# One product for v of both head pairs, the gate's rank-16 input in fp32 quarters, and attention of both pairs chunk by chunk

## The chip, the cores and the metric

The kernel runs on one core of a Trainium2 chip. The metric is the device time of one execution in microseconds (us); lower is better. A core has a matrix engine (TensorE, PE in the rows; PEld is its weight load), a vector engine (VectorE, DVE), an activation engine (ScalarE, ACT), GpSimd (POOL) and a queue that issues most DMAs (SyncE, SP). They run beside each other and wait for each other through semaphores. Each engine takes its own instructions strictly in the order in which the program lists them.

## The reference

One layer of a decoder runs over 1024 prompt tokens and 64 sample tokens (8 sequences of 8), 1088 in all. The part that the change touches is gated linear attention, with 4 heads of key width 64 and value width 128:

```python
h = rms_norm(x, norm_g)
proj = jnp.einsum('btd,de->bte', h, w_in.astype(h.dtype))
a, gl, zc, q, k, v, zg, lr = jnp.split(proj, SPLIT_POINTS, axis=-1)
u = a * jax.nn.sigmoid(gl)                       # then a causal depthwise conv, width 31, over u
...
gk = jax.nn.log_sigmoid((jnp.einsum('btr,rk->btk', lr, w_alpha.astype(lr.dtype))
                         + b_alpha.astype(lr.dtype)).astype(jnp.float32)) / GATE_NORM
...                                              # per chunk of tokens, with state S:
bcum = jnp.cumsum(gi, axis=-2)
q_t = qi * jnp.exp(bcum)
k_t = ki * jnp.exp(-bcum)
attn = jnp.where(mask, jnp.einsum('bhtd,bhsd->bhts', q_t, k_t), 0.0)
o = jnp.einsum('bhtd,bhdv->bhtv', q_t, S) + jnp.einsum('bhts,bhsv->bhtv', attn, vi)
S = S * jnp.exp(b_last)[..., None] + jnp.einsum('bhsd,bhsv->bhdv', k_dec, vi)
```

`lr` has 16 columns, `v` has 512, `q` and `k` have 256 each.

## The kernel before, in words

Tokens stand in three chunks of 384, 384 and 320 columns; in the last one 256 are prompt and 64 sample tokens. A matrix product of full accuracy is made of three products in the fast format fp32r: operands are split into a high part `h_` (a copy on ACT) and a low part `l_` (a subtraction on DVE, `split`, L422), and TensorE adds high by high, high by low and low by high. Plain fp32 products are slower and show as two matrix records in the trace.

The work in program order: projections `gl` and `a` of four channel tiles (PSUM tiles `p_gl`, `p_a`); `v` for head pair 0 by nine token tiles (`v_tile`, PSUM `pv`), in which 16 more columns give `lr`; `q` and `k` of pair 0 by chunk with its attention between them; `v` of pair 1; `q`, `k` and attention of pair 1; `zc`, `zg`, the pointwise product `pw` and the output products `ya`, `yc`, `pys`.

`lr` of a token tile is copied into `lrst`, its low part subtracted, transposed by TensorE (`lrtp`, L690) and copied to `lrT`. `gates` (L705) multiplies it by `was` (PSUM `pg`), takes the log-sigmoid on ACT and DVE, a cumulative sum on DVE (`scan`, L718) into `B`, and then exponentials on ACT into `ep` and `em`. `q_chunk` and `k_chunk` multiply these by q and k. `gla_states` (L765) transposes k (`pk`, copied to `kT`), multiplies by v (`px`) and updates the state. `gla_out` (L797) makes the attention matrix (`pa`), masks it (DVE `select`, tile `at`) and adds state and attention products in `po`.

The causal convolution is 31 taps for each of four channel tiles, each tap one DVE instruction over 1024 columns (`cv`, L562), and for the sample tokens 31 small ACT instructions and two DVE reductions per tile (L575, L576). `conv_tick(n)` puts the next n of them into the program at low priority.

The order on each engine is not written by hand: `Program.schedule` runs the list of operations against costs written in the code and takes, whenever an engine is free, the ready operation of lowest number (low-priority ones last). What it decides is fixed in the program; the chip then keeps that order, whatever things really take. Its costs for a reduction and a cumulative sum are those of plain element work:

```python
prog.add("DVE", lambda: V.tensor_tensor_scan(R(out), R(a), R(b), 0.0, ALU.mult, ALU.add), [out], [a, b],
         out.n / 0.96 + 67)
...
prog.add("DVE", lambda: V.tensor_reduce(R(out), R(a), mybir.AxisListType.X, ALU.add), [out], [a],
         a.n / 0.96 + 67)
```

Of the kernel before, what the change touches and what calls it, by code (L numbers as in the profile page):

```python
# [48 lines left out]
ADD_LAG = 5000  # L49
SQ_SUM = (2, 4, 8)  # L50
# [76 lines left out]
class Op:  # L127
    __slots__ = ("eng", "fn", "cost", "lag", "table", "prio", "seq", "deps", "users", "wait", "ready", "tiles",
                 "allocs", "start", "end", "bytes", "name")


class Program:
# [9 lines left out]
    def add(self, eng, fn, outs, ins, cost, table=None, nbytes=0, lag=0):  # L142
        o = Op()
        o.eng, o.fn, o.cost, o.table, o.bytes, o.lag = eng, fn, cost, table, nbytes, lag
        o.seq = len(self.ops)
# [37 lines left out]
    def schedule(self):  # L183
# [26 lines left out]
        done = []  # L210

        def can_alloc(o, t):
            need = {}
            for tl in o.tiles:
                if tl.tag in free_at and tl.slot is None:
                    need.setdefault(tl.tag, []).append(tl.first)
            for tag, firsts in need.items():
                have = sum(1 for f in free_at[tag] if f <= t)
                before = min(bisect_left(pend[tag], min(firsts)), self.reserve.get(tag, 1 << 30))
                if have < len(firsts) + before:  # L220
                    return False
            return True
# [6 lines left out]
        while events:  # L229
# [3 lines left out]
            best = None  # L233
            nxt = None
            for o in avail[e]:
                if o.ready <= t:
                    if (best is None or o.prio < best.prio) and can_alloc(o, t):
                        best = o
                elif nxt is None or o.ready < nxt:
# [71 lines left out]
def build(tc, A, O):  # L311
# [3 lines left out]
    prog = Program({"big": NBIG, "unit": NUNIT, "wst": NST, "wl": NW, "wh": NW, "ps": 8, "kT": 2, "S": 6, "ss": 9},  # L315
                   {"ps": 3, "unit": 6, "big": 2})
# [68 lines left out]
    def mm(ps, lhsT, rhs, start, stop, after=(), pair=False):  # L385
# [3 lines left out]
        o = prog.add("PE", lambda: T.matmul(R(ps), R(lhsT), R(rhs), start=start, stop=stop, skip_group_check=True),  # L389
                     [ps], [lhsT, rhs], c / 2 if pair else c, lag=lag)  # L390
# [6 lines left out]
    def transpose(out, in_, idn):  # L397
        return prog.add("PE", lambda: T.transpose(R(out), R(in_), R(idn)), [out], [in_, idn], 109)

    with ctx:  # L400
# [43 lines left out]
        lrst = [VT(fixed, f"lrst{i}", [P, P], F32, f"lrst{i}") for i in range(2)]  # L444
        u_s = [VT(fixed, f"us{i}", [P, NB, CW - 1 + LB], F32, f"us{i}") for i in range(CT)]
        v_s = VT(fixed, "vs", [P, 256], F32, "vs")
# [7 lines left out]
        for t_ in at_p + [at_s] + lrst:  # L454
# [171 lines left out]
        def packed(name, ps, terms):  # L626

            n = len(terms)
            for i, (both, hi, w_h, w_l) in enumerate(terms):
                mm(ps, both, w_h, i == 0, False)  # L630
                mm(ps[0:64], hi, w_l, False, i == n - 1)
            t_ = un(f"half_{name}")
            act(t_[0:64, :ps.n], ps[64:128], AF.Copy)
            return t_


        vt = [[None] * NTT, [None] * NTT]
        lrT = [None] * 3
        hp = VT(big, "big", [P, KT, P], F32R, "hp")

        def v_weights(p):
            cols = 272 if p == 0 else 256
            return cols, [load_split(f"v{p}{i}", A[f"wv{p}"][i], 2, cols) for i in range(4)]

        def v_tile(p, w, tk):
            cols, w = w
            rows = P if tk < 8 else 64
            c = min(tk // 3, 2)
            off = tk * P - CHUNKS[c][0]
            ts_ = slice(off, off + rows)  # L650
            if tk < 8:
                if tk % 4 == 0:
                    vt[p][tk] = VT(big, "big", [P, 4, 256], F32, f"v{p}_{tk}")
                vt[p][tk] = v = vt[p][tk - tk % 4] if tk % 4 else vt[p][tk]
                v = v[:, tk % 4, :]
            else:
                vt[p][8] = v = v_s
            ps = pt(f"pv{p}_{tk}")
            o = ps[:rows, :cols]
            terms = []  # L660
            src = ps[:rows, 256:272]
            if tk < 8:
                for k in range(KT):
                    hi, lo = w[k // 2]
                    terms += [(hh[k][c][:, ts_], hi[:, k % 2, :]), (hh[k][c][:, ts_], lo[:, k % 2, :]),
                              (hl[k][c][:, ts_], hi[:, k % 2, :])]
                accumulate(o, terms)
                act(v[:rows], ps[:rows, 0:256], AF.Copy)
            else:
                for k in range(KT):  # L670
                    hi, lo = w[k // 2]
                    if p == 0:
                        act(hp[:, k, 0:64], hh[k][c][:, 256:320], AF.Copy)
                        act(hp[:, k, 64:128], hl[k][c][:, 256:320], AF.Copy)
                    terms.append((hp[:, k, :], hp[:, k, 0:64], hi[:, k % 2, :], lo[:, k % 2, :]))
                half = packed(f"pv{p}", ps[:, :cols], terms)
                tt(v[:rows], ps[:rows, 0:256], half[:rows, 0:256], ALU.add)
                if cols > 256:
                    tt(half[:rows, 256:272], src, half[:rows, 256:272], ALU.add)
                    src = half[:rows, 256:272]  # L680
            if cols > 256:
                st = lrst[tk % 2]
                sv = st.split(64)
                for a in range(2):
                    act(sv[:rows, a, 0:16].bitcast(F32R), src, AF.Copy)
                for a in range(2):
                    tt(sv[:rows, a, 32:48].bitcast(F32R), src, sv[:rows, a, 0:16], ALU.subtract)
                if off == 0:
                    lrT[c] = un(f"lrT{c}", F32R)
                tp = pt(f"lrtp{tk}")  # L690
                transpose(tp[:, :rows], st[:rows, :], ident[:rows, :rows])
                act(lrT[c][:, ts_], tp[:, :rows], AF.Copy)

        def vslice(p, tk):
            return vt[p][tk][:, tk % 4, :] if tk < 8 else v_s
# [9 lines left out]
        def gates(p, c):  # L705
            t0, n = CHUNKS[c]
            pg = pt(f"pg{p}_{c}")
# [9 lines left out]
            B = un(f"B{p}_{c}")  # L717
# [13 lines left out]
            for i in range(np_):  # L731
                ss_ = slice(i * P, i * P + P)
                act(ep[:, ss_], B[:, ss_], AF.Exp, scale=GN, bias=g_nm[p][:, i0 + i:i0 + i + 1])
                act(em[:, ss_], B[:, ss_], AF.Exp, scale=-GN, bias=g_m[p][:, i0 + i:i0 + i + 1])
            act(g_c[p][:, lo:i0 + np_], g_c[p][:, lo:i0 + np_], AF.Exp)
            if c == 2:
                Bs = B[:, m:n].split(LB)
                act(ep[:, m:n], B[:, m:n], AF.Exp, scale=GN)
                act(em[:, m:n], B[:, m:n], AF.Exp, scale=-GN)
                act(g_c[p][:, 8:9], g_d[p][:, 7:8], AF.Exp)  # L740
                act(g_c[p][:, 12:20], Bs[:, :, LB - 1], AF.Exp, scale=GN)
# [23 lines left out]
        def gla_states(p, c):  # L765
# [3 lines left out]
            km = gx[(p, c)][1]  # L769
            pk = pt(f"pk{p}_{c}")  # L770
            for i in range(nt):
                transpose(pk[:, P * i:P * i + P], km[:, P * i:P * i + P], ident)
            kT = un(f"kT{p}_{c}")
            act(kT[:, :m], pk[:, :m], AF.Copy)
# [637 lines left out]
```

## Time and profile before

| what | value |
|---|---|
| median of 3 runs | 470.25 us (469.52 to 470.39) |
| profiled execution, its own time | 470.04 us |
| its span, first to last instruction | 467.9 us |
| TensorE busy | 458.9 us, 98% of the span |
| VectorE busy | 401.1 us, 86% |
| ScalarE busy | 304.4 us, 65% |

The profile is one execution, taken on the core. Busy times of TensorE count overlapping matrix products as one stretch, and the ends of products are modelled, so the pace of a run of products is read from their starts or from the chain of waits. The 2.1 us between the span and the time of the same execution lie outside the instructions.

### The profile page before, as it was taken

To read this page: it belongs to the slowest core of one execution; us is meant where nothing else is said; L and a number is where in the kernel's file an instruction comes from. 1 tells how busy PE (TensorE), PEld (TensorE's weight loads), DVE (VectorE), ACT (ScalarE), POOL (GpSimd) and SP (SyncE) were. 2 spreads that over 40 slices of the span, in tenths; PEclk is the share of its full clock that TensorE was granted. 3 is DMA by queue.
4 is the path that set the end of the run, shared out by engine and by line. 5 is a ranking of instruction groups with operands and counts; after the bars stand their busy time and mean duration, and the time that the engine had idled before them with its cause. 6 is when DMAs were issued, how large, how long until landed. Compare 5 with 4: busy or idle time off the path is not lost.

```text
span 467.9 us, 7864 instructions
## 1 busy us (share of the span) xinstructions
PE 458.9 (98%) x2867; PEld 431.2 (92%) x2867; DVE 401.1 (86%) x634; ACT 304.4 (65%) x780; POOL 19.3 (4%) x39
## 2 busy tenths in 40 slices
PE   8999999999999999999999999999999999999994
PEld 7899999999999999999999999999999988888783
DVE  4999998999999989999888999995548848988674
ACT  6978649926670545685634696544899548878636
POOL 1000000000000000000000000000000023130000
PEclk9999999999999999999999999999999999999998
DMA  8910283313012110022021011102235392386754
GB/s 253 352 57 1 93 205 57 54 51 69 1 59 78 36 56 6 35 73 77 20 71 39 14 47 45 46 22 73 88 78 181 87 228 48 68 182 154 242 174 179
DMA packets 33238, 43.28 MB, mean 92 GB/s; under 512 B 11696, under 2 KB 16560, under 8 KB 33200
## 3 DMA queue, kind: packets, MB, share of 16 engines
q1 hardware_dynamic: 30896, 38.59, 26.5%
q0 software_dynamic: 2304, 4.20, 5.5%
q8 instruction: 22, 0.36, 0.3%
q14 instruction: 16, 0.13, 0.1%
HBM read 36.58 MB, written 6.19 MB: 91 GB/s over the span
## 4 chain that ended last, share of the span: by engine, by line
PE 88%; DMA 4%; DVE 3%; ACT 3%; issue 1%; SPq 1%; DVEq 0%
PE pv L389 11%; PE p_zc L389 10%; PE p_zg L389 10%; PE p_gl L389 8%; PE p_a L389 8%; PE ya L389 7%; PE p_k L389 5%; PE p_q L389 5%; PE pw L389 5%; PE yc L389 5%; PE po L389 2%; PE pys L389 2%; DMA xr<-in_x 1%; DVE xr L343 1%; DMA s_gl<-in_w_in 1%; DMA s_a<-in_w_in 1%
## 5 line engine op out<-in xcount | busy, mean ns | idle before, releaser
L339 DVE SCALAR_TENSOR_TENSOR cv<-u,par,cv 128x1024 f32<-128x1024 f32 x120 | 150.8, 1278 | 0.2
L389 PE MATMUL pv<-h_v,hh 128*128 128x272 f32 (+1 forms) x128 | 37.4, 292 | 0.0
L389 PE MATMUL pv<-h_v,hl 128*128 128x272 f32 (+1 forms) x128 | 37.1, 290 | 0.0
L389 PE MATMUL pv<-l_v,hh 128*128 128x272 f32 (+1 forms) x128 | 36.8, 288 | 0.0
L333 ACT ACTIVATE pr<-us,par 128x64 f32<-128x64 f32 x124 | 32.3, 343 | 2.4 <-DMA us<-in_cc 2.4
L389 PE MATMUL p_gl<-hh,h_gl 128*128 128x384 f32 (+1 forms) x96 | 32.5, 339 | 0.8 <-ACT hh L333 0.8
L389 PE MATMUL p_zc<-hh,h_zc 128*128 128x384 f32 (+1 forms) x96 | 32.0, 333 | 0.0
L389 PE MATMUL p_gl<-hl,h_gl 128*128 128x384 f32 (+1 forms) x96 | 31.7, 330 | 0.2 <-DVE hl L343 0.2
L389 PE MATMUL p_a<-hh,l_a 128*128 128x384 f32 (+1 forms) x96 | 31.8, 331 | 0.0
L389 PE MATMUL p_a<-hh,h_a 128*128 128x384 f32 (+1 forms) x96 | 31.5, 328 | 0.1
L389 PE MATMUL p_zc<-hh,l_zc 128*128 128x384 f32 (+1 forms) x96 | 31.5, 329 | 0.0
L389 PE MATMUL p_zc<-hl,h_zc 128*128 128x384 f32 (+1 forms) x96 | 31.5, 328 | 0.0
L389 PE MATMUL p_gl<-hh,l_gl 128*128 128x384 f32 (+1 forms) x96 | 31.5, 328 | 0.0
L389 PE MATMUL p_zg<-hh,l_zg 128*128 128x384 f32 (+1 forms) x96 | 31.5, 328 | 0.0
L389 PE MATMUL p_zg<-hl,h_zg 128*128 128x384 f32 (+1 forms) x96 | 31.4, 327 | 0.0
L389 PE MATMUL p_zg<-hh,h_zg 128*128 128x384 f32 (+1 forms) x96 | 31.4, 327 | 0.0
L389 PE MATMUL p_a<-hl,h_a 128*128 128x384 f32 (+1 forms) x96 | 31.4, 327 | 0.0
L389 PEld LDWEIGHTS pv<-h_v,hh 128*128 128x128 f32 x128 | 24.1, 188 | 0.6 <-issue 0.2
L389 PEld LDWEIGHTS pv<-h_v,hl 128*128 128x128 f32 x128 | 24.1, 188 | 0.3 <-issue 0.3
L389 PEld LDWEIGHTS pv<-l_v,hh 128*128 128x128 f32 x128 | 24.1, 189 | 0.2
L389 PEld LDWEIGHTS p_gl<-hh,h_gl 128*128 128x128 f32 x96 | 18.1, 189 | 1.7 <-ACT hh L333 1.2
L389 PEld LDWEIGHTS p_gl<-hl,h_gl 128*128 128x128 f32 x96 | 18.2, 189 | 0.9 <-DVE hl L343 0.5
(337 smaller groups left out, 1306.8 us busy)
## 6 DMA issues: line engine op xcount, KB each, us to landing
xr<-in_x SPq DMA_DIRECT2D x16, 256.0 KB, 4.4
out_y<-xr SPq DMA_DIRECT2D x16, 256.0 KB, 2.3
x<-in_xT SPq DMA_DIRECT2D x16, 192.0 KB, 4.5
T<-in_w_out POOLq DMA_DIRECT2D x12, 256.0 KB, 5.1
s_gl<-in_w_in SPq DMA_DIRECT2D x8, 256.0 KB, 4.9
s_a<-in_w_in SPq DMA_DIRECT2D x8, 256.0 KB, 4.1
s_zc<-in_w_in SPq DMA_DIRECT2D x8, 256.0 KB, 2.6
s_zg<-in_w_in SPq DMA_DIRECT2D x8, 256.0 KB, 2.7
```

Source lines behind the costliest of these rows:

```text
L333: return S.activation(R(out), R(in_), func, **kw)
L339: return prog.add("DVE", lambda: V.scalar_tensor_tensor(R(out), R(a), R(s), R(b), op0, op1), [out], [a, s, b], out.n / 0.96 + 67 + 62 * is ...
L343: return prog.add("DVE", lambda: V.tensor_tensor(R(out), R(a), R(b), op), [out], [a, b], out.n / 0.96 + 67)
L389: o = prog.add("PE", lambda: T.matmul(R(ps), R(lhsT), R(rhs), start=start, stop=stop, skip_group_check=True), [ps], [lhsT, rhs], c / 2 if ...
```

## The change

There are four parts.

1. **v in one product.** `v_tile` makes v of both pairs at once, 512 columns per product, in place of 272 (pair 0 with `lr`) and 256 (pair 1). The weights are eight tiles of 512 columns, each loaded by two DMAs.
2. **The gate input.** `gate_rank` computes `lr` in plain fp32: for each of 8 row blocks four products with 32 weight columns (16 of them zero) and 272 token columns, one for each quarter of the tokens, into four groups of 32 PSUM partitions (`pl`). Its weights come by four DMAs of 64-byte runs into `lr_w`. `gate_rows` copies the result to `lrT` by ACT. The 9 transposes and the `lrst` copies are gone.
3. **Attention by chunk.** `gla_states` handles both pairs, `gla_out` and the gates of both pairs follow chunk by chunk, and what was pair 1's later work moves ahead, among `zc`. More convolution taps stand among the v tiles (`conv_tick(4)`).
4. **The order.** The scheduler knows for each TensorE operation whether it is fp32 or fp32r (`kind`), charges 90 ns for a change, and stays with the kind that runs where a ready operation of it is less than `STICK = 60` numbers behind. An fp32r product is charged 14 ns beside its columns, not 2.5.

```diff
+STICK = 60
...
+            if same is not None and same.prio < best.prio + STICK:
+                best = same
...
+            if e == "PE" and o.kind != kind[0]:
+                kind[0] = o.kind
+                cost += 90
...
-    prog = Program({"big": NBIG, "unit": NUNIT, "wst": NST, "wl": NW, "wh": NW, "ps": 8, "kT": 2, "S": 6, "ss": 9},
-                   {"ps": 3, "unit": 6, "big": 2})
+    prog = Program({"big": NBIG, "unit": NUNIT, "wst": NST, "wl": NW, "wh": NW, "ps": 8, "kT": 2, "S": 8, "ss": 9},
+                   {"ps": 3, "unit": 8, "big": 2})
...
-        c = max(n / 2.4 + 2.5, m / 1.2) if R_DT(rhs) else max(n / 1.2 + 2.5, m / 1.2) + max(n / 1.2 if m > 64 else 53, m / 1.2)
+        c = max(n / 2.4 + 14, m / 1.2) if R_DT(rhs) else max(n / 1.2 + 2.5, m / 1.2) + max(n / 1.2 if m > 64 else 53, m / 1.2)
...
+        def gate_rank():
+            w = un("lr_w")[:, 0:256].split(32)
+            prog.hold = True
+            zero(w)
+            for i in range(4):
+                dma(w[:, 2 * i:2 * i + 2, 0:16], A["wv0"][i][:, :, 256:272], late=True)
+            pl = pt("pl")[:, :QT]
+            for k in range(KT):
+                for g in range(4):
+                    mm(pl[32 * g:32 * g + 32], w[:, k, :], rows("x", k, F32)[:, QT * g:QT * g + QT],
+                       k == 0, k == KT - 1, share=4)
+            th, tl = un("lr_h", F32R)[:, :QT], un("lr_l", F32R)[:, :QT]
+            split(th, tl, pl)
...
+                for p in range(2):
+                    dma(st[:, 256 * p:256 * p + 256], A[f"wv{p}"][k // 2][:, k % 2, 0:256])
...
+        gate_rank()
         for ct in (2, 3):
...
+        wv = v_weights()
         for tk in range(NTT):
+            v_tile(wv, tk)
+            conv_tick(4)
+            if tk in (3, 6):
+                gates(tk // 3 - 1, 0)
+        wqk = [(wtile("q", p), wtile("k", p)) for p in range(2)]
+        for c in range(3):
+            for p in range(2):
                 if (p, c) not in gx:
                     gates(p, c)
+            for p in range(2):
+                q_chunk(p, wqk[p][0], c)
                 conv_tick(2)
                 if c > 0:
+                    if p == 0:
+                        gla_states(c - 1)
+                    else:
+                        gla_out(1, c - 1)
+                k_chunk(p, wqk[p][1], c)
                 conv_tick(2)
+                if c > 0 and p == 0:
+                    gla_out(0, c - 1)
```

Where the scheduler then puts things is seen in the built programs. The first place is, on TensorE, the middle of `p_gl2_1`, the second chunk of the projection `gl` of channel tile 2 (`hh`, `hl` are the split activations, `h_gl2`, `l_gl2` the split weights). Before:

```order
L389 MATMUL p_gl2_1_838<-hl3_203,h_gl2_0_630 128x384
L389 MATMUL p_gl2_1_838<-hh3_187,l_gl2_0_691 128x384
L389 MATMUL p_gl2_1_838<-hh4_210,h_gl2_1_657 128x384
L389 MATMUL p_gl2_1_838<-hl4_228,h_gl2_1_657 128x384
L389 MATMUL p_gl2_1_838<-hh4_210,l_gl2_1_700 128x384
```

and in the change:

```order
L403 MATMUL p_gl2_1_841<-hl3_199,h_gl2_0_626 128x384
L403 MATMUL p_gl2_1_841<-hh3_183,l_gl2_0_672 128x384
L403 MATMUL pl_861<-x0_88,lr_w_790 32x272 x4
L403 MATMUL pl_861<-x1_92,lr_w_790 32x272 x4
L403 MATMUL pl_861<-x2_96,lr_w_790 32x272 x4
L403 MATMUL pl_861<-x3_100,lr_w_790 32x272 x4
L403 MATMUL pl_861<-x4_108,lr_w_790 32x272 x4
L403 MATMUL pl_861<-x5_110,lr_w_790 32x272 x4
L403 MATMUL pl_861<-x6_112,lr_w_790 32x272 x4
L403 MATMUL pl_861<-x7_116,lr_w_790 32x272 x4
L403 MATMUL p_gl2_1_841<-hh4_205,h_gl2_1_655 128x384
```

All 32 products `pl` now stand after the first 36 of the 72 products of `gl2`, and the rest of TensorE's work stands behind them. The weights `lr_w` come through the SP queue, whose rows at that time (`us` are the sample tokens' conv caches, `cst` constants, `s_v` staged weights of v) were, before:

```order
L377 DMA us3_795<-in_cc 128x8x30
L377 DMA cst_798<-in_cst 128x960
L377 DMA bm_800<-in_bm 64x8
L377 DMA cst2_802<-in_cst2 128x384
L377 DMA s_v03_818<-in_wv0 128x544
```

and are in the change:

```order
L391 DMA us3_798<-in_cc 128x8x30
L391 DMA cst_800<-in_cst 128x960
L391 DMA bm_803<-in_bm 64x8
L391 DMA cst2_805<-in_cst2 128x384
L391 DMA lr_w_790<-in_wv0 128x2x16 x4
L391 DMA s_v3_820<-in_wv0 128x256
L391 DMA s_v3_820<-in_wv1 128x256
```

The four loads stand in the place of the fourth v load, behind the four conv caches and the constants. The second place is just ahead of the first q product. ACT and DVE make its weights `h_q0_0`, `l_q0_0`; before, DVE's rows there were taps alone (`cv`), while TensorE was still in `gl3`:

```order
L339 SCALAR_TENSOR_TENSOR cv1_830<-u1_294,par_86,cv1_830 128x1024
L339 SCALAR_TENSOR_TENSOR cv0_727<-u0_381,par_86,cv0_727 128x1024
L343 TENSOR_TENSOR l_q0_0_1202<-s_q0_0_945,h_q0_0_1190 128x512
L339 SCALAR_TENSOR_TENSOR cv0_727<-u0_381,par_86,cv0_727 128x1024
L343 TENSOR_TENSOR l_q0_1_1226<-s_q0_1_969,h_q0_1_1208 128x512
```

In the change DVE has the cumulative sum of pair 1's first gates (`ge1_0<-cst,g1_0`) and taps ahead of it:

```order
L353 SCALAR_TENSOR_TENSOR cv1_894<-u1_287,par_86,cv1_894 128x1024
L368 SCALAR_TENSOR_TENSOR ge1_0_1673<-cst_800,g1_0_1680 128x384
L353 SCALAR_TENSOR_TENSOR cv1_894<-u1_287,par_86,cv1_894 128x1024
L353 SCALAR_TENSOR_TENSOR gd1_1717<-ge1_0_1673,gm1_1708 128x3
L353 SCALAR_TENSOR_TENSOR cv2_1494<-u2_985,par_86,cv2_1494 128x1024
L357 TENSOR_TENSOR gc1_1731<-gd1_1717,gm1_1708 128x2
L357 TENSOR_TENSOR l_q0_0_1733<-s_q0_0_1291,h_q0_0_1719 128x512
```

and ACT has what follows from that sum ahead of `h_q0_0`:

```order
L347 ACTIVATE gnm1_1705<-ge1_0_1673 128x3
L347 ACTIVATE gm1_1708<-ge1_0_1673 128x3
L347 ACTIVATE g1_0_1680<-ge1_0_1673,gm1_1708 128x128 x2
L347 ACTIVATE h_q0_0_1719<-s_q0_0_1291 128x512
L347 ACTIVATE g1_0_1680<-ge1_0_1673,gm1_1708 128x128
L347 ACTIVATE h_q0_1_1727<-s_q0_1_1377 128x512
```

The q weights moved from a place in which nothing waited for them soon to one right behind the gates, with the first q product next on TensorE.

The third place is the end of the program, where the last four token tiles (`xr4` to `xr7`, halves `_0` and `_1`) are added to the output products (`ya`), squared and summed on ACT (`ss`) and scaled (the instruction with `fg`). DVE's last rows before:

```order
L343 TENSOR_TENSOR xr5_0_4977<-ya1_4439,xr5_0_4977 128x512
L339 SCALAR_TENSOR_TENSOR xr4_0_4975<-xr4_0_4975,ss4_5055,fg_4416 128x512
L339 SCALAR_TENSOR_TENSOR xr5_0_4977<-xr5_0_4977,ss5_5061,fg_4416 128x512
L343 TENSOR_TENSOR xr6_0_4979<-ya2_4456,xr6_0_4979 128x512
L343 TENSOR_TENSOR xr7_0_4982<-ya3_4470,xr7_0_4982 128x512
```

and in the change:

```order
L353 SCALAR_TENSOR_TENSOR xr4_0_4742<-xr4_0_4742,ss4_4793,fg_4181 128x512
L357 TENSOR_TENSOR xr5_0_4744<-ya1_4204,xr5_0_4744 128x512
L353 SCALAR_TENSOR_TENSOR xr5_0_4744<-xr5_0_4744,ss5_4827,fg_4181 128x512
L357 TENSOR_TENSOR xr6_0_4746<-ya2_4221,xr6_0_4746 128x512
L357 TENSOR_TENSOR xr7_0_4748<-ya3_4235,xr7_0_4748 128x512
```

The addition for tile 5 now stands behind the scaling of tile 4, no longer ahead of it; the additions for tiles 6 and 7 stand as before.

## Rows read from the trace of the kernel before

**Rows 1.** The page: busy time and share of the span, by engine.

```profile
PE 458.9 (98%) x2867; PEld 431.2 (92%) x2867; DVE 401.1 (86%) x634; ACT 304.4 (65%) x780; POOL 19.3 (4%) x39
```

**Rows 2.** A window: length, then busy (instructions) of PE, PEld, DVE, ACT, POOL; clock.

```profile
60.00:108.00 48.00, 48.00 (x293) 48.00 (x292) 46.19 (x47) 30.87 (x110) 0.00 (x0) 1.00 0.39 79
```

**Rows 3.** Chain of waits: start us, us, what, number; the first v stretch.

```profile
108.24 5.67 PE pv L389 x45
113.91 0.11 PE lrtp L398
```

**Rows 4.** Chain of waits over the whole span, three long pieces.

```profile
60.70 11.90 PE p_gl L389 x72
...
197.14 2.84 PE pv L389 x24
...
390.21 10.88 PE ya L389 x48
```

**Rows 5.** Timeline of PE (start, length, what, number) around a state product.

```profile
149.64 0.34 PE L389 MATMUL p_k<-hh,l_k 128*128 128x384 f32 x1
149.91 0.88 PE L389 MATMUL px<-v,kT 128*64 128x128 f32 x12
150.72 0.44 PE L389 MATMUL p_k<-hh,h_k 128*128 128x384 f32 x1
151.00 0.34 PE L389 MATMUL p_k<-hl,h_k 128*128 128x384 f32 x1
```

**Rows 6.** Timeline of SP's queue; start us and us of the issue.

```profile
60.25 4.29 SPq L377 DMA_DIRECT2D us<-in_cc  x4
...
66.55 0.38 SPq L377 DMA_DIRECT2D s_v<-in_wv  x1
```

**Rows 7.** DMA issues from 58 to 80 us: number, size, median us to landing.

```profile
s_v<-in_wv SPq DMA_DIRECT2D x3, 272.0 KB, 2.8
...
us<-in_cc SPq DMA_DIRECT2D x4, 120.0 KB, 4.3
...
bm<-in_bm SPq DMA_DIRECT2D x1, 2.0 KB, 3.8
```

**Rows 8.** Timeline of DVE: taps, a cumulative sum, splits, a reduction, a tap.

```profile
101.69 3.67 DVE L339 SCALAR_TENSOR_TENSOR cv<-u,par,cv 128x1024 f32<-128x1024 f32 x3
...
134.32 0.95 DVE L354 TENSOR_TENSOR_SCAN B<-cst,g 128x384 f32<-128x384 f32 x1
135.19 1.27 DVE L343 TENSOR_TENSOR l_v<-s_v,h_v 128x512 fp32r<-128x512 f32 x2
...
142.36 1.97 DVE L364 TENSOR_REDUCE pr<-pr 128x64 f32<-128x1024 f32 x1
144.25 1.27 DVE L339 SCALAR_TENSOR_TENSOR cv<-u,par,cv 128x1024 f32<-128x1024 f32 x1
```

**Rows 9.** Timeline of ACT: exponentials of the gates, a copy of transposed k.

```profile
138.52 0.39 ACT L333 ACTIVATE ge<-B,gnm 128x128 f32<-128x128 f32 x1
138.82 0.39 ACT L333 ACTIVATE g<-B,gm 128x128 f32<-128x128 f32 x1
...
148.96 0.49 ACT L333 ACTIVATE kT<-pk 128x384 f32<-128x384 f32 x1 [9.17 <-PE pk L398]
```

**Rows 10.** Windows at the end; the last figures are clock, DMA share, GB/s.

```profile
460.90:463.60 2.70, 0.15 (x1) 0.00 (x0) 1.37 (x3) 2.51 (x10) 0.00 (x0) 1.00 0.50 191
463.70:467.90 4.20, 0.00 (x0) 0.00 (x0) 0.63 (x1) 0.60 (x1) 0.00 (x0) 0.50 0.54 208
```

**Rows 11.** Timeline of the end: ACT and DVE on the last token tiles.

```profile
455.69 0.63 ACT L333 ACTIVATE sq<-xr 128x512 bf16<-128x512 f32 x1 [0.60 <-DVE xr L343]
...
456.30 0.68 DVE L343 TENSOR_TENSOR xr<-ya,xr 128x512 f32<-128x512 f32 x1
...
457.01 0.75 DVE L339 SCALAR_TENSOR_TENSOR xr<-xr,ss,fg 128x512 f32<-128x512 f32 x1
...
459.61 0.68 DVE L343 TENSOR_TENSOR xr<-ya,xr 128x512 f32<-128x512 f32 x1
```

More of the change, by code (lines that the diff above doesn't have):

```diff
@@ L128 @@
     __slots__ = ("eng", "fn", "cost", "lag", "table", "prio", "seq", "deps", "users", "wait", "ready", "tiles",
-                 "allocs", "start", "end", "bytes", "name")
+                 "allocs", "start", "end", "bytes", "name", "kind")
 class Program:
@@ L232, in schedule @@
                 continue
-            best = None
+            best = same = None
             nxt = None
@@ L238, in schedule @@
                         best = o
+                    if (e == "PE" and o.kind == kind[0] and (same is None or o.prio < same.prio)
+                            and can_alloc(o, t, True)):
+                        same = o
                 elif nxt is None or o.ready < nxt:
@@ L397, in transpose @@
     def transpose(out, in_, idn):
-        return prog.add("PE", lambda: T.transpose(R(out), R(in_), R(idn)), [out], [in_, idn], 109)
+        return prog.add("PE", lambda: T.transpose(R(out), R(in_), R(idn)), [out], [in_, idn], 109, kind=False)
     with ctx:
@@ L641, in v_weights @@
[L641 to L647, printed above, removed]
+        QT = NTOK // 4
+        lr_parts = []
+        def gate_rank():
[11 more added lines that the diff above has]
+            split(th, tl, pl)
+            lr_parts.extend((th, tl))
@@ new lines, in build, with gate_rows @@
+        lrT = [None] * 3
+        def gate_rows(c):
+            t0, n = CHUNKS[c]
+            lrT[c] = un(f"lrT{c}", F32R)
+            for g in range(4):
+                a, b = max(t0, QT * g), min(t0 + n, QT * g + QT)
+                if a < b:
+                    for i in range(4):
+                        act(lrT[c][32 * i:32 * i + 32, a - t0:b - t0],
+                            lr_parts[i % 2][32 * g:32 * g + 32, a - QT * g:b - QT * g].bitcast(F32), AF.Copy)
+        vt = [None] * NTT
@@ new lines, in build, with v_weights @@
+        hp = VT(big, "big", [P, KT, P], F32R, "hp")
+        def v_weights():
+            out = []
+            for k in range(KT):
+                st = VT(wst, "wst", [P, 512], F32, f"s_v{k}")
+                hi = VT(wh, "wh", [P, 512], F32R, f"h_v{k}")
+                lo = VT(wl, "wl", [P, 512], F32R, f"l_v{k}")
+                for p in range(2):
+                    dma(st[:, 256 * p:256 * p + 256], A[f"wv{p}"][k // 2][:, k % 2, 0:256])
+                split(hi, lo, st)
+                out.append((hi, lo))
+            return out
@@ L648, in v_tile @@
+        def v_tile(w, tk):
             c = min(tk // 3, 2)
             off = tk * P - CHUNKS[c][0]
-            ts_ = slice(off, off + rows)
+            ts_ = slice(off, off + P)
+            ps = pt(f"pv{tk}")
             if tk < 8:
[L652 to L657, printed above, removed]
@@ L675, in v_tile @@
[L675 to L692, printed above, removed]
+                    act(hp[:, k, 0:64], hh[k][c][:, 256:320], AF.Copy)
@@ L1070, in build @@
+        for i in range(4):
+            w = wtile("zc", i)
+            for c in range(3):
+                zc_chunk(i, w, c)
+                conv_tick(5)
+                for f, *args in beside[(i, c)]:
+                    f(*args)
         conv_tick(1000)
```

207 lines of the change are left out of this document (86 added, 121 removed).

## The prediction

> **What bounds the kernel now.** I read the page's busy times first. TensorE is busy for 98% of the span, VectorE for 86% [rows 1]. In a window of the middle, 60 to 108 us, TensorE has no gap at all while VectorE is busy for 46.2 of 48 us [rows 2]: TensorE sets the end, and VectorE runs just behind it with almost no slack. So work taken off TensorE counts in full, and a new wait of TensorE counts in full as well, which VectorE can cause as soon as its work is put in another order. The chain of waits gives the pace of TensorE's products, with long runs of one kind in it. A product of 272 columns takes 5.67/45 = 0.126 us [rows 3], one of 256 2.84/24 = 0.118, one of 512 10.88/48 = 0.227, and `p_gl`, whose chunks are 384, 384 and 320 wide, 11.90 us for 72, in proportion 0.174 for 384 columns and 0.146 for 320 [rows 4]. A plain fp32 transpose of 128 columns stands between two fp32r runs with 0.11 us [rows 3]; no time for a change of precision shows there.
>
> The timeline around a `px` block tells where changes do cost. The block is six fp32 products of 128 by 64, twelve records; from the `p_k` ahead of it to the second one behind it are 151.00 - 149.64 = 1.36 us [rows 5], less two `p_k` of 0.174 leaves 1.01. Twelve records one after the other would take 12 x 0.11 = 1.3 by the transpose, so the two halves run side by side: six steps, 0.66 us, and 0.35 for going into narrow products and out again. The Trainium skill has a rule for that (TensorEngine Tiling (Array Packing), section Key Properties): changing the tiling mode drains TensorE. It is a rule on shapes, not on precision, and the two rows agree with it: 0.35 us around narrow products, nothing seen around the full-size transpose.
>
> **The change part by part.** The sum is made against the profiled execution's own 470.04 us (span 467.9), 0.2 below the median of 470.25.
>
> v in one product: 208 products (192 of the full token tiles, 16 of the last) at 0.227 in place of 208 pairs at 0.126 + 0.118. That is 208 x 0.0175 = -3.6 us, all on TensorE. Bounds -2.6 and -4.6, 5 ns either way on a product.
>
> Transposes of `lr`: eight of full size at 0.11, -0.9.
>
> Attention of both pairs together, and the order that keeps to one precision: precision changes on TensorE fall from 103 to 47 in the built programs, and blocks of narrow products from 24 to 16 beside `pl`. By what these rows show only the blocks count [rows 3, 5]: 8 x 0.35 = -2.8. Below this stands 0, if drains are only moved; above it, if every change costs half a block's 0.35, 56 x 0.175 = -9.8.
>
> `pl` is new: 32 products of 32 output columns over 272 columns of fp32. A step of `px` (one record of each of the two halves, 128 columns) takes 0.11 us by the split above, so a step of 272 columns takes 0.11 x 272/128 = 0.23. If four run at once there are 16 steps (two records each of eight row blocks), 3.7 us, and one block's 0.35: +4.0. Two at a time give +7.7, one at a time 15. I take four, as the two halves of `px` are seen side by side. The Trainium skill speaks against a full factor of four (TensorE: Matmul & The Clock Gate, section Measured speedup vs the span model): three narrow column tiles gained 2.38 and not 3; in proportion `pl` would come to an estimated 4.6 and 0.35, or +4.9, for which no row here stands. TensorE's work is thus -3.6 - 0.9 - 2.8 + 4.0 = -3.3.
>
> The wait at `pl`. It stands behind 36 products of `gl2`: from 60.70 us [rows 4] 36 x 0.174 = 6.3, so TensorE comes to it at 67.0. Its weights `lr_w` are queued on SP behind four cache loads that take 4.3 us to issue, and constants; where they now stand, a v load was issued at 66.55 [rows 6], and one more load half ahead of the caches adds its 0.38 us, so 66.9. Small runs land late: the 2 KB of `bm` after 3.8 us, the caches, of 120-byte runs, after 4.3, the big v loads after 2.8 [rows 7]. `lr_w` has 64-byte runs and is small; I take 3.8, and the first of the four loads lets TensorE start. TensorE waits 66.9 + 3.8 - 67.0 = +3.7 (bounds 2.7 and 4.3 by these rows, 0 if the load gets ahead). Everything behind `pl` on TensorE waits with it, and so does VectorE, whose split of `lr` is in its queue.
>
> The wait at the first q product. From the end of `pl` TensorE has the rest of `gl2` (12 x 0.174 + 24 x 0.146 = 5.6), `a2`, `gl3`, `a3` (3 x 11.9 = 35.7), v (208 x 0.227 = 47.2) and 0.7 for two `pg` and two q products: 89.2 us. VectorE, which must make `l_q0_0` for the third q product, has in its new order 58 taps, four reductions, nine splits, two cumulative sums and 18 smaller instructions between its split of `lr` and `l_q0_0`. From one start to the next a tap takes (3.67 - 1.27)/2 = 1.2, a split 0.6 (two in 1.27), the cumulative sum 0.87 (134.32 to 135.19), the reduction 1.89 (142.36 to 144.25) [rows 8]: 69.3 + 7.6 + 5.4 + 1.7, and some 0.34 for each small one, 6.1, together 90.1 us. It starts about 1 us after `pl`, and 0.2 us pass before TensorE sees the result: +2.1 of waiting. The planner's cost for a reduction is 1.13 and for a sum 0.47; that is why it saw none. With ACT the q weight's high part is queued behind the exponentials' offsets that wait for that sum, which is part of the same 2.1. Bounds 0 and 5 (3% of VectorE's 90 us either way).
>
> The wait at the first state product. TensorE has 146 products of 0.174, two `pg` and six transposes, 26.4 us, from the third q product to `px0_0`. VectorE has ten taps, eight splits, two reductions and some eight smaller ones to the end of the next cumulative sum, 25.5. ACT then has six exponentials at 0.30 (138.52 to 138.82), 0.4 for the long one and 0.3 of small ones, and the copy `kT` of 0.49, which is queued behind them [rows 9]; with 0.4 of latencies 28.9. +2.5; bounds 0 and 4.
>
> Later waits of the same kind (a select ahead of the first `po`, the norm of the first outputs): +1.5 by the same counts, bounds 0 and 3. From there VectorE has the slack of the later stages.
>
> The end. Before, the addition for tile 5 started at 456.30 beside ACT's square of tile 4 (455.69); the scaling of tile 4 came at 457.01. Now that addition follows the scaling: 457.01 + 0.65 = 457.66, 1.4 us later. From an addition to ACT's square behind it pass 0.7, from the square to the scaling 1.32 (455.69 to 457.01), to the next addition 0.65: the addition for tile 6 comes at 460.33, where it was at 459.61 [rows 11]. ACT's chain behind it is the last one, so +0.7 (bounds 0 and 1.4).
>
> Sum: -3.3 + 3.7 + 2.1 + 2.5 + 1.5 + 0.7 = +7.2, so 477.2 on the profiled execution, 477.5 on the median.
>
> **Rivals.** B, the clock falls while TensorE waits. At the end it was at its high level for 2.7 us after the last product and at half from 463.7 [rows 10], while TensorE did nothing; a wait of 3.7 at `pl` is longer than that. No row shows how long it takes to rise again; the row at half covers the last 4.2 us, and as much work at half clock would lose half of that, +2.1: 479.6. Against it: that fall came behind the end of all work, and it would come only just before `lr_w` lands here. The Trainium skill's page on the clock gate (section HAM oscillation — how this bites in real kernels) says that waits for DMAs can throw the clock back each time, which would be this case; no row of before has such a wait.
>
> C, `lr_w` lands in time, since small transfers pass the caches: without 3.7, 473.8.
>
> D, `pl` goes two at a time: +3.7, 481.2.
>
> E, VectorE keeps up (its order has 1% less in it than I count, and the other waits with it): without 2.1 + 2.5 + 1.5, 471.4.
>
> F, the other side: each change of precision costs half of 0.35, whatever the shape. 56 fewer are -9.8 in place of -2.8: 470.5, no change; above 0.2 a change it would be faster. The transpose at 0.11 speaks against it [rows 3].
>
> **How the numbers follow.** A, as summed, 0.36; B 0.24; C 0.10; D 0.07; E 0.10; F 0.05; C and E together (467.7) 0.06; rest 0.02. The time is A's, 477.5. The range goes from E, 471.5, to D, 481.3, which leaves out F, C with E and parts of E and D. A measurement of this kernel can tell about 0.2% (0.94 us) from no change: faster 0.09, same 0.06, slower 0.85.
>
> **What would show it.** In the profile after: `pl` with idle time ahead of it that a DMA `lr_w` ends (3.7), and about 4 us long; v at 0.227 a product in one run of 47 us; idle time of TensorE ahead of `p_q` ended by ACT or VectorE (2.1) and ahead of `px` ended by `kT` (2.5); narrow blocks of both pairs as one; a granted clock under 1.0 behind `pl` for B. The prediction is wrong if TensorE shows no gaps, or if `pl` takes 8 us, or if the full-size blocks turn out to cost what the narrow ones do.

## The result and the profile after

The change makes the kernel slower by more than was forecast: 483.02 us median of 4 runs (482.08 to 488.16) against 469.88 for the kernel before beside it; ratio over all these runs 1.0306, interval 1.023 to 1.0381 (the medians alone give 1.028). The prediction was 477.5, its range ended at 481.3. The profiled execution took 483.29 us with a span of 481.5, 13.6 more than the span of before.

The page's row of busy times, which answers to [rows 1], says at once what kind of loss it is:

```profile
PE 459.8 (95%) x2714; PEld 420.0 (87%) x2714; DVE 397.7 (83%) x615; ACT 306.8 (64%) x769; POOL 19.5 (4%) x38
```

TensorE is busy as long as before (458.9 there), in a span that is 13.6 us longer: it waits. What it waits for is a view of its own (engine, line, what ended the wait: us in total, times, longest):

```profile
PE pl L403 <- DMA lr_w<-in_wv: 3.1, 1, 3.1
PE p_q L403 <- ACT h_q L347: 1.9, 1, 1.9
...
PE on_1p L403 <- DVE on_1l L357: 0.9, 1, 0.9
PE p_q L403 <- DVE l_q L357: 0.9, 1, 0.9
PE px L403 <- ACT kT L347: 0.9, 1, 0.9
...
PE ya L403 <- DVE xr L357: 0.7, 1, 0.7
PE po L403 <- DVE at L375: 0.4, 1, 0.4
```

The forecast places are there: `pl`, q (`p_q`), `px`, and the later ones (`po` behind the select, `on_1p` for the norm of the first outputs). Two more are not forecast: `ya` in the last stage and a small one at `pj_3p`, which isn't shown (0.3). The timeline of TensorE around three of them (columns as in [rows 5]; in brackets idle time and what ended it) lets one measure each from start to start:

```profile
66.49 0.34 PE L403 MATMUL p_gl<-hh,l_gl 128*128 128x384 f32 x1
69.96 5.26 PE L403 MATMUL pl<-x,lr_w 128*32 128x272 f32 x64 [3.14 <-DMA lr_w<-in_wv]
75.15 0.44 PE L403 MATMUL p_gl<-hh,h_gl 128*128 128x384 f32 x1
...
166.22 0.44 PE L403 MATMUL p_q<-hh,h_q 128*128 128x384 f32 x1 [1.93 <-ACT h_q L347]
...
167.75 0.44 PE L403 MATMUL p_q<-hh,l_q 128*128 128x384 f32 x1 [0.92 <-DVE l_q L357]
...
196.83 0.88 PE L403 MATMUL px<-v,kT 128*64 128x128 f32 x12 [0.90 <-ACT kT L347]
```

From 66.49 to 69.96 are 3.47 us, less one product of 0.17: 3.3 of waiting, 3.7 forecast. (The view of waits counts from the modelled end of the last product, and so shows a little less.) `pl` takes 5.19 us, 4.0 forecast. The two waits at q are 2.1 and 1.1, `px` is late by 1.05 more. The granted clock (the last figures but two, after the busy times) explains `pl`, and a slow stretch behind the waits at q:

```profile
68.50:69.00 0.50, 0.00 (x0) 0.00 (x0) 0.50 (x1) 0.00 (x0) 0.00 (x0) 1.00 0.48 75
69.50:70.00 0.50, 0.04 (x4) 0.07 (x6) 0.50 (x1) 0.33 (x2) 0.00 (x0) 0.50 0.20 19
72.50:73.00 0.50, 0.50 (x12) 0.25 (x8) 0.00 (x0) 0.00 (x0) 0.00 (x0) 0.67 1.03 137
168.00:172.00 4.00, 4.00 (x15) 4.00 (x15) 4.00 (x6) 3.59 (x9) 0.00 (x0) 0.57 0.36 131
```

It stands at half (1.2 in place of 2.4 GHz) from 69.5 on, late in the pause, until some way into `pl` at 72.8, and again in most of 168 to 172 (0.57 over 4 us is 3.4 us at half, 1.7 lost). In the kernels below in which `pl` keeps the high clock it takes 3.8 us.

The end grew most. DVE's last additions and scalings (those that answer to [rows 11]):

```profile
467.47 0.68 DVE L357 TENSOR_TENSOR xr<-ya,xr 128x512 f32<-128x512 f32 x1
469.51 0.75 DVE L353 SCALAR_TENSOR_TENSOR xr<-xr,ss,fg 128x512 f32<-128x512 f32 x1 [1.35 <-ACT ss L347]
470.18 0.68 DVE L357 TENSOR_TENSOR xr<-ya,xr 128x512 f32<-128x512 f32 x1
472.21 0.75 DVE L353 SCALAR_TENSOR_TENSOR xr<-xr,ss,fg 128x512 f32<-128x512 f32 x1 [1.35 <-ACT ss L347]
...
476.84 0.75 DVE L353 SCALAR_TENSOR_TENSOR xr<-xr,ss,fg 128x512 f32<-128x512 f32 x1 [1.18 <-ACT ss L347]
```

The order is as forecast: the addition for tile 5 (470.18) behind the scaling of tile 4 (469.51), 2.71 us from one tile to the next. From the addition for tile 4 (467.47) to the last scaling (476.84) are 9.4 us, before 8.6 (454.98 to 463.58): 0.8 more, 0.7 forecast. But the addition for tile 4 now starts 3.4 us ahead of TensorE's last product; before it was 5.7. These are DVE's two rows of before, and TensorE's last rows before and after (the last product starts 0.39, its own length, ahead of the end of its row: 460.66 and 470.83):

```profile
454.98 0.68 DVE L343 TENSOR_TENSOR xr<-ya,xr 128x512 f32<-128x512 f32 x1
463.58 0.75 DVE L339 SCALAR_TENSOR_TENSOR xr<-xr,ss,fg 128x512 f32<-128x512 f32 x1 [1.14 <-ACT ss L333]
450.01 11.04 PE L389 MATMUL ya<-p4b,p4a 128*128 128x512 f32 x48
462.76 8.46 PE L403 MATMUL ya<-p4b,p4a 128*128 128x512 f32 x36 [0.67 <-DVE xr L357]
```

From the last product to the end of the span are 10.7 us, before 7.2. Of the 3.4 more, 0.8 are thus the order, 2.3 the later start against TensorE, 0.3 stand behind the last scaling.

So the 13.6 us: from the start of `gl2` (0.1 earlier than before) to the last product TensorE takes 410.4 us in place of 400.1, and the end 3.4 more. In the 10.3 are 10.4 us of waits (3.3, 2.1, 1.1, 1.05, 0.5 at `po`, 1.1 at `on_1p`, 0.8 at `ya`, 0.45 at `pj_3p`), 1.4 and 1.7 of low clock. What remains is -3.2 for TensorE's own work, -3.3 forecast. The kernel of experiment 8 bears this out: 398.1 us over the same stretch with 1.4 of waiting, so 3.4 of work less than before.

### The profile page after: what moved, and what is told of

Same layout as the page of the kernel before. It is cut to its first block, busy times and chain, and to the rows that moved or that the text cites. A ratio compares the mean times of both kernels' runs of the same rounds, so it can differ in the third digit from the quotient of the medians.

```text
span 481.5 us, 7536 instructions
## 1 busy us (share of the span) xinstructions
PE 459.8 (95%) x2714; PEld 420.0 (87%) x2714; DVE 397.7 (83%) x615; ACT 306.8 (64%) x769; POOL 19.5 (4%) x38
## 4 chain that ended last, share of the span: by engine, by line
PE 51%; DVE 32%; ACT 6%; issue 4%; DMA 3%; SPq 2%; DVEq 0%
DVE cv L353 16%; PE p_zg L403 10%; PE ya L403 8%; PE p_zc L403 8%; PE pw L403 5%; PE yc L403 5%; DVE x L353 2%; PE p_k L403 2%; PE po L403 2%; SPq L391 2%; DVE pr L378 2%; DVE cv L378 2%; PE pys L403 2%; DVE hl L357 2%; PE p_q L403 1%
## 5 line engine op out<-in xcount | busy, mean ns | idle before, releaser
L403 PE MATMUL pv<-h_v,hl 128*128 128x512 f32 x64 | 24.9, 390 | 0.0
L403 PE MATMUL pv<-l_v,hh 128*128 128x512 f32 x64 | 24.9, 389 | 0.0
L403 PE MATMUL pv<-h_v,hh 128*128 128x512 f32 x64 | 24.9, 389 | 0.0
L357 DVE TENSOR_TENSOR o<-o,zg 128x384 f32<-128x384 f32 (+1 forms) x12 | 6.2, 532 | 15.8 <-ACT zg L347 15.8
L403 PEld LDWEIGHTS p_a<-hh,h_a 128*128 128x128 f32 x96 | 18.0, 188 | 1.0 <-ACT h_a L347 1.0
L403 PEld LDWEIGHTS p_gl<-hh,l_gl 128*128 128x128 f32 x96 | 18.0, 188 | 0.6 <-DVE l_gl L357 0.4
```

The source lines that it names most:

```text
L357: return prog.add("DVE", lambda: V.tensor_tensor(R(out), R(a), R(b), op), [out], [a, b], out.n / 0.96 + 67)
```

## The experiments

All times are medians beside runs of the kernel before on the same chip (469.7 to 470.0). The planner is `Program.schedule`; waits are read behind 28 us. Theory from the traces: VectorE is the bound from `pl` to `px`, and the order of its work comes from one number of the planner. Rivals: the load at `pl` and the clock carry the loss; the gates' new place or the rule on precision makes the waits.

**1. The load earlier.** Only SP's order is changed.

```diff
         order = self.schedule()
+        first = next(i for i, o in enumerate(order) if o.eng == "SP" and o.tiles[0].name == "us0")
+        moved = [o for o in order[first:] if o.eng == "SP" and o.tiles[0].name == "lr_w"]
+        order = order[:first] + moved + [o for o in order[first:] if o not in moved]
```

> The changed kernel with its four lr_w loads moved ahead of the four cache loads on SP, every other order kept. Theory (the products pl wait for lr_w, and the pause of TensorE drops its clock to half): pl starts right behind gl2, with no wait (3.3 us less) and at the high clock throughout, 3.5 us long in place of 5.2 (1.7 less); all work behind it comes 5.0 us earlier, 478.0 in place of 483.0. Rival (the low clock in pl has another cause): pl stays 5.2 long, 479.7. Rival (the cache loads, now later, are waited for in turn): no gain, 482 to 483.

483.42 us, ratio 1.0281 (1.0248 to 1.0314): no gain, though the wait at `pl` is gone and `pl` runs at the high clock in 3.8 us. The waits have moved (the two longest in the view of waits, as above):

```profile
PE pv L406 <- DVE l_v L360: 3.3, 2, 2.0
PE px L406 <- ACT kT L350: 2.5, 1, 2.5
```

So the load and the clock at `pl`, which the expectation had as its theory, don't carry the loss by themselves. Why, the two timelines show, ACT's:

```profile
72.71 0.31 ACT L350 ACTIVATE Jr<-cst 128x128 fp32r<-128x128 f32 x1 [7.01 <-DMA cst<-in_cst]
...
75.36 0.38 ACT L350 ACTIVATE lr_h<-pl 128x272 fp32r<-128x272 f32 x1
```

and DVE's:

```profile
75.77 0.44 DVE L360 TENSOR_TENSOR lr_l<-pl,lr_h 128x272 fp32r<-128x272 f32 x1 [4.96 <-ACT lr_h L350]
```

`pl` ends at 71, but ACT's copy `lr_h` of it stands in ACT's queue behind the copy of `Jr`, which waits for the constants, 3 us later than in the changed kernel, and behind ten short instructions more; so VectorE starts on `lr_l` at 75.77. In the changed kernel it does so at 75.72, when `pl` has ended at 75.15:

```profile
75.72 0.44 DVE L357 TENSOR_TENSOR lr_l<-pl,lr_h 128x272 fp32r<-128x272 f32 x1 [5.33 <-ACT lr_h L347]
```

That two different causes end so close to each other is chance. And `px` starts at 196.87 here, 196.83 there, 121.1 us after `lr_l` in both, though TensorE stands at other places in between:

```profile
196.87 0.88 PE L406 MATMUL px<-v,kT 128*64 128x128 f32 x12 [2.48 <-ACT kT L350]
```

**2 and 3. Products in the pauses.** In two kernels spare products, whose results nothing uses, keep TensorE busy in the pause ahead of `pl`, or in the two ahead of q; they wait for nothing new. In the second kernel they alter q's first chunk, so its output is another.

```diff
+        def pad(o, out, n):
+            real, m = o.fn, out.n
+            def fn():
+                for i in range(n):
+                    x = T.matmul(R(out), R(rows("hh", 0, F32R)[:, 0:P]), R(rows("hh", 1, F32R)[:, 0:m]), start=True, stop=True,
+                                 skip_group_check=True)
+                    first = x if i == 0 else first
+                real()
+                return first
+            o.fn = fn
...
+                    if k == g == 0:
+                        pad(prog.last_pe, pl, 25)
...
+                    if name == "q0" and c == 0 and k == 0 and i != 1:
+                        pad(prog.last_pe, ps[:, 384:512], 30 if i == 0 else 14)
```

> The changed kernel with 25 spare products (272 columns, into pl's own PSUM bank ahead of its first product) in the wait ahead of pl; the wait for lr_w itself stays. Theory (the clock falls because TensorE pauses): the granted clock stays at 1.00 there, pl starts as before and takes 3.5 us, 1.7 less: 481.3. Rival (the clock falls for another reason, or the fall costs nothing because VectorE is the bound from there on): 483.0.

> The changed kernel with 30 and 14 spare products of 128 columns (into unused columns of the PSUM bank) in the two waits ahead of the first and the third q product. Theory (VectorE is the bound from pl to the first state product px): the clock stays at 1.00 behind the waits, TensorE comes to px 1.7 us earlier, and waits there 2.7 us in place of 1.0: no gain, 483.0. Rival (TensorE is the bound again behind the q wait): 1.7 less, 481.3.

The first took 482.5 us, 1.0269 (1.0238 to 1.0301), the second 482.57, 1.0271 (1.0232 to 1.0311): neither differs from the changed kernel. In the first the clock held and `pl` took 3.8 us, but in that execution the loads were issued 1.1 us later (67.57 against 66.49) and `pl` started 1.0 later, so `lr_l` came only 0.4 earlier (DVE, then TensorE):

```profile
75.31 0.44 DVE L357 TENSOR_TENSOR lr_l<-pl,lr_h 128x272 fp32r<-128x272 f32 x1 [3.87 <-ACT lr_h L347]
```

```profile
196.43 0.88 PE L403 MATMUL px<-v,kT 128*64 128x128 f32 x12 [0.91 <-ACT kT L347]
```

In the second the pause ahead of `pl` was not filled, and this time the clock didn't fall in it (its windows from 66.9 to 70 and behind q):

```profile
66.90:70.00 3.10, 0.16 (x1) 0.00 (x1) 3.06 (x4) 0.27 (x2) 0.00 (x0) 1.00 0.65 193
168.00:172.00 4.00, 4.00 (x25) 4.00 (x25) 4.00 (x6) 2.38 (x5) 0.00 (x0) 1.00 0.33 104
```

`lr_l` came 1.3 us earlier than in the changed kernel, and `px` too (DVE, then TensorE):

```profile
74.39 0.44 DVE L357 TENSOR_TENSOR lr_l<-pl,lr_h 128x272 fp32r<-128x272 f32 x1 [3.77 <-ACT lr_h L347]
```

```profile
195.50 0.88 PE L403 MATMUL px<-v,kT 128*64 128x128 f32 x12 [0.94 <-ACT kT L347]
```

The second kernel is no clean test of the clock behind q: the clock held, but the spare products ran past the pauses. The third q product starts at 168.03, 2.3 us behind the start of DVE's split `l_q` (165.70), in the changed kernel 0.7 (167.75, 167.02). These 1.6 us are about what the clock gave back, so TensorE's wait at `px` stayed at 1.1 us where 2.7 were expected. The clean case is experiment 1: there the clock is high behind q, TensorE waits 2.65 us at `px` (start to start), and `px` comes no earlier. From `lr_l` to `px` are 121.11 us in the changed kernel, 121.10, 121.12 and 121.11 in these three, whatever TensorE does between.

**4. Three taps less.** VectorE's last three taps ahead of its first instruction on `g1_0` (pair 1's first gates) are left out, so the convolution of one channel tile lacks three taps.

```diff
+        dve = [o for o in order if o.eng == "DVE"]
+        at = next(i for i, o in enumerate(dve) if any(t.name == "g1_0" for t in o.tiles))
+        out = dve[at - 3:at]
...
+        order = [o for o in order if o not in out]
```

> The changed kernel without the last three convolution taps ahead of the second gates (3 x 1.2 us of VectorE; the convolution of one channel tile lacks three taps), every order kept. Theory (VectorE, not the load at pl, sets the time of the first q product and of the first state product px): the waits ahead of q shrink from 3.2 us to nothing and px comes 3.6 us earlier, as does all behind it: 479.4. Rival (ACT's order or the load at pl is what TensorE waits for): px and the end stay, 483.

480.36 us, 1.0216 (1.0193 to 1.0239). `lr_l` and `px` (DVE, then TensorE):

```profile
75.87 0.44 DVE L362 TENSOR_TENSOR lr_l<-pl,lr_h 128x272 fp32r<-128x272 f32 x1 [5.55 <-ACT lr_h L352]
```

```profile
193.39 1.16 PE L408 MATMUL px<-v,kT 128*64 128x128 f32 x12 [2.24 <-ACT kT L352]
```

117.52 us: 3.59 less, three taps of 1.2. The waits at q are gone, the one at `px` is 2.2; the span is 3.3 shorter. VectorE's queue is shown to be the bound there: work taken out of it, and nothing else, brings `px` forward by as much.

**5. The planner's number.** Two kernels with one number exchanged: the change with 2.5 ns, and the kernel before with 14.

```diff
-        c = max(n / 2.4 + 14, m / 1.2) if R_DT(rhs) else ...
+        c = max(n / 2.4 + 2.5, m / 1.2) if R_DT(rhs) else ...
```

> The changed kernel with one number of the planner put back: an fp32r product is charged 2.5 ns beside its columns and not 14. Theory (the higher charge lets the planner put more VectorE work, taps above all, ahead of what TensorE needs, and so makes the waits at q, px, the norms and in the tail): these waits go, 3.2 + 1.0 + 1.9 + 4.0 = 10.1 us; the wait at pl (2.6 to 3.4) with its low clock stays: 473 (471 to 475). Rival (the order comes from keeping to one precision and from the gates' new place): waits and time stay, 481 to 485.

471.8 us, 1.0043 (1.0023 to 1.0064): one number gives back 11.2 of the 13.1 us. One wait of TensorE is left, and the end is 7.1 us again, from the last product at 461.91 (windows):

```profile
PE pl L403 <- DMA lr_w<-in_wv: 2.2, 1, 2.2
```

```profile
462.00:469.00 7.00, 0.30 (x2) 0.00 (x0) 2.10 (x3) 2.79 (x7) 0.00 (x0) 0.90 0.45 170
```

SP's timeline shows a step of the long end: the eight loads of `xr` for the last tiles start 22.2 us ahead of the last product (461.91) here,

```profile
439.69 3.94 SPq L391 DMA_DIRECT2D xr<-in_x  x8
```

18.8 ahead of it (470.83) in the changed kernel and 21.4 (460.66) in the kernel before:

```profile
452.07 4.16 SPq L391 DMA_DIRECT2D xr<-in_x  x8
439.22 4.31 SPq L377 DMA_DIRECT2D xr<-in_x  x8
```

From there to DVE's addition for tile 4 pass 15.4 to 15.8 us in all three. In the chain of work that ended last, the changed kernel leaves TensorE at 453.95 for one of these loads and the additions behind it, the kernel before at 439.30; with 2.5 ns in the change it stays on TensorE to the last product (chain: after, before, this kernel):

```profile
454.61 6.07 DMA xr<-in_x
441.78 6.61 DMA xr<-in_x
440.38 21.93 PE ya L403 x96
```

> The kernel before with one number of the planner as in the change: an fp32r product is charged 14 ns beside its columns and not 2.5. Theory (this number alone makes TensorE look slower in the plan, so that VectorE gets more taps ahead of what TensorE waits for): TensorE waits for VectorE in the v stretch and at the attention, several us in all, about 477 (474 to 481). Rival (the waits come from the gates' new place, not from the number): 470, no change.

481.41 us, 1.0247 (1.022 to 1.0274): the number alone, without any other part of the change, costs 11.7 us, more than was expected of it. TensorE waits at other places, behind VectorE's queue all the same, and the end is as long as in the change (view of waits, DVE, windows). The longest wait, put down to "issue", ends at 116.43, behind the low part `lrst`, which DVE makes at 116.07 after taps and a split:

```profile
PE lrtp L398 <- issue: 3.4, 1, 3.4
PE lrtp L398 <- DVE lrst L343: 1.4, 2, 0.7
```

```profile
116.07 0.25 DVE L343 TENSOR_TENSOR lrst<-pv,lrst 128x16 fp32r<-128x16 f32 x2
```

```profile
469.60:479.80 10.20, 0.20 (x1) 0.00 (x0) 3.45 (x5) 5.59 (x15) 0.00 (x0) 0.72 0.54 206
```

**6. VectorE's costs as measured.**

```diff
         prog.add("DVE", lambda: V.tensor_tensor_scan(R(out), R(a), R(b), 0.0, ALU.mult, ALU.add), [out], [a, b],
-                 out.n / 0.96 + 67)
+                 out.n * 2.1 + 67)
...
         prog.add("DVE", lambda: V.tensor_reduce(R(out), R(a), mybir.AxisListType.X, ALU.add), [out], [a],
-                 a.n / 0.96 + 67)
+                 a.n * 1.77 + 67)
```

> The changed kernel with the planner's cost of a reduction at 1.88 us and of a cumulative sum at 0.87, as the trace shows them; the 14 ns stays. Theory (the plan saw no wait at q and px because these two were charged 0.8 and 0.4 us too little each): the waits ahead of q, px, the select and the norm go, 7 to 8 us; the tail keeps its 3 to 4 us more: 475.5 (474 to 478). Rival (these costs are too few to matter, the taps' place is set by the 14 ns): 481 to 483.

476.43 us, 1.0138 (1.0123 to 1.0153). With the 14 ns kept and these two right, the waits at q are gone, and the end is still 10.7 us; the waits left over 0.5 us:

```profile
PE pl L403 <- DMA lr_w<-in_wv: 2.6, 1, 2.6
PE ya L403 <- DVE xr L357: 1.0, 1, 1.0
PE px L403 <- ACT kT L347: 0.7, 1, 0.7
```

**7. The rank-16 product later.** With 2.5 ns, `gate_rank()` is called between `gl2` and `a2`.

```diff
-        gate_rank()
         for ct in (2, 3):
...
+            if ct == 2:
+                gate_rank()
             for c in range(3):
                 a_chunk(ct, wa_, c)
```

> The changed kernel with the 2.5 ns charge and with the rank-16 product asked for behind gl2, not ahead of it. Theory (with the charge back only the wait for lr_w is left, 2.3 us, and 36 products of gl2 more in front of pl cover it): no gap of TensorE over 0.5 us behind 30 us, 469.5 (468.5 to 470.5), against 471.8 with the charge alone. Rival (the load lands as late relative to pl as before, since it is issued later too): 471.8.

467.85 us, 0.9954 (0.9941 to 0.9967): faster than both kernels. The view of waits behind 28 us:

```profile
PE pl L403 <- DMA lr_w<-in_wv: 0.6, 1, 0.6
PE ya L403 <- DVE xr L357: 0.5, 1, 0.5
```

It is 1.65 us faster than expected, below the stated range, and the wait isn't quite covered. More than the wait is gained: the products of v take 47.3 us here and 48.4 in the first kernel of 5, at the full clock in both. Why they are slower there no run shows.

**8. Without the rule on precision**, on top of that kernel.

```diff
-STICK = 60
+STICK = -10 ** 9
-                cost += 90
+                cost += 0
```

> The kernel of the last comparison (charge of 2.5 ns, rank-16 product behind gl2) without the planner's rule on precision: no charge of 90 ns for a change and no staying with one kind. TensorE changes precision 71 times in place of 49, with 18 blocks of narrow products in place of 19. Theory (only going into narrow products and out costs, a change of precision by itself nothing): 467.9, no difference (467 to 469). Rival (each change costs the 90 ns of the planner): 22 x 0.09 = 2.0 more, 469.8.

467.69 us, 0.9947 (0.9933 to 0.9962), against 467.85 in 7: 22 more changes of precision cost nothing that can be measured, where 2.0 us were the rival's. The 90 ns of the planner's rule aren't seen on the chip.

**9. Two mixtures.** The 2.5 ns with the load ahead of the caches (the edits of 5 and 1); and the later product with VectorE's true costs and 14 ns (7 and 6).

> The changed kernel with the 2.5 ns charge and with the lr_w loads ahead of the cache loads. Theory (the pause at pl goes, but ACT's copy of lr is still queued behind what the late caches and constants release, so VectorE pauses as long as before and TensorE gets back at most a part): 470.5 (469.5 to 471.8). Rival (with the charge back TensorE is the bound everywhere, so the pause at pl counts in full): 469.5 or less.

470.14 us, 1.0 (0.9984 to 1.0015): part of the gain of 7, the number as expected. The reason is another: the view of waits has none of TensorE here, so VectorE's pause doesn't reach it. TensorE needs 400.1 us from `gl2` to the last product all the same (1.1 more than in 7 in v alone, as in 5), and why is open.

> The changed kernel with the rank-16 product behind gl2 and reductions and sums charged as measured; the 14 ns charge stays. Theory (the longer tail comes from the order that the 14 ns gives to the last weights' splits, not from the waits ahead of it): no gap over 1 us in the middle, the tail still 10 us from the last product to the end in place of 7, 473.5 (472 to 475). Rival (the tail was late because VectorE was late before it): tail 7 us, 469 to 470.

473.62 us, 1.0083 (1.0058 to 1.0109); the profiled execution, at 470.67, was the shortest of four. TensorE has one wait over 0.5 us (1.1 at `px`), its last product starts at 458.29, as early as in the fastest kernels, and yet the end takes 10.6 us (windows):

```profile
458.50:468.90 10.40, 0.17 (x1) 0.00 (x0) 3.45 (x5) 5.45 (x15) 0.00 (x0) 0.71 0.53 200
```

The long end thus doesn't follow from the waits before it; it comes with the 14 ns in all eight kernels planned with it (10.4 to 10.7 us from the last product's start to the end), and with 2.5 ns it is 7.1 to 7.7 (before and the four others). In these eight the `xr` loads start 18.2 to 19.4 us ahead of the last product and the addition for tile 4 3.3 to 3.5; in the five others 21.4 to 22.2 and 5.6 to 7.0. What in the plan of the last stage the number shifts was followed only that far: that the late loads make the late additions is read from the chain and the order of rows, and a kernel with only that stage's order put back wasn't tried.

## Why the prediction was wrong

The direction and the mechanism stood: new waits of TensorE behind VectorE's order outweigh the work saved. Two sizes didn't: the end, which failed, and the clock, which the sum put at nothing.

- **TensorE's work** was forecast at -3.3 and is -3.2 (what remains of the sum). v takes 47.3 us (47.2 forecast), `pl` at the high clock 3.8 (4.0): the four narrow column tiles do run side by side, as the halves of `px` do, and the 4.9 estimated by the Trainium skill's figure for three (TensorE: Matmul & The Clock Gate, section Measured speedup vs the span model) was too much. Changes of precision cost nothing that can be measured (experiment 8), as [rows 3] had it and against rival F; the Trainium skill's sentence on draining at a change of tiling mode (TensorEngine Tiling (Array Packing), section Key Properties) fits this, with 71 changes no slower than 49 at about as many blocks.
- **The wait at `pl`** is 3.3 (3.7 forecast). Rival B came true in this execution: the clock fell and cost 1.4 in `pl`. It had 0.24 and was put behind A.
- **From `pl` to `px`** the sum held: 120.2 us were forecast (1 + 90.1 to the q weight, 0.2, 28.9), 121.7 measured from the end of `pl` at 75.15 to 196.83. The waits at q are 3.2 in place of 2.1 and at `px` 1.05 in place of 2.5, because the second fall of the clock took 1.7 us out of that wait (where the clock is high behind q, experiment 1, it is 2.65). So waits of one chain were added up rightly only since VectorE was counted through; the load and the clock matter there by what they do to the start of `lr_l`, and not by TensorE's idle time (experiments 1 to 4).
- **The end** is the step that failed, the last term of the sum: +0.7 forecast, 3.4 measured, and 0.8 ahead of `ya`. The order of tiles 4 to 7 was costed rightly (0.8 us, 2.7 a tile); but the start was taken from before. The loads of `xr`, queued on SP behind outputs, start 2.7 us later against TensorE's last product than in the kernel before, and the additions behind them 2.3 later (experiment 5 and the profile after). The prediction looked at the last five rows of DVE and not at what stands ahead of them. This term and 0.8 are 3.5 of the 6.4 us between 7.2 and 13.6; 1.9 are the later `px` (1.2 of it in `pl`), 0.5 the later waits, 0.5 the rest.
- **The cause of the orders** wasn't named: the prediction read the orders as given and passed over the charge of 14 ns that makes them. It is the better value (a 512-column product takes 227 ns, 213 and 14), and it makes the plan worse, in the kernel before too (experiment 5). Part of the reason is that the plan's VectorE is too fast by 0.75 us at each reduction and 0.4 at each sum: with these right the change takes 6.6 us less (experiment 6). That holds for the waits; the long end stays (experiments 6 and 9), and why the number makes it is open.

## What to carry to other kernels

In a kernel whose second engine is nearly full, look for the chain that runs through that engine before adding up the waits of the first: here the four kernels with the same order on VectorE came to `px` 121.1 us after VectorE had `lr_l`, and idle time of TensorE in between was worth nothing. A planner's costs work together: here the right cost of one engine let another's errors decide, so read the order that follows, to the end of the program. And a load that is moved up takes its place in front of others: see who waits for those.

## What was not expected of the hardware

The length of a pause alone did not decide whether the clock fell: it fell in the pause of 3.3 us ahead of `pl` in the changed kernel and of 3.2 in experiment 4, and held in one of 3.1 with the same orders ahead of it (the second kernel of 2 and 3) and in 2.4 and 2.8 (experiments 5 and 6). Behind one of 2.4, ahead of `px` in experiment 4, it fell (to half from 193.8 on). The Trainium skill says of the start of a kernel that the same program shows different numbers of slow products from run to run (TensorE: Matmul & The Clock Gate, Part 1, section What's actually happening); here a fall that comes in one execution and not in another is seen in the middle, in kernels alike up to that point. Where VectorE was the bound behind it, the fall brought `px` no later (experiment 1 against the changed kernel).
